# 192 tokens gather their experts and 320 are dense, in a layer whose PEER experts were split 128 to 384; gathered v rows come a token at a time and are summed by TensorE

## The chip, the cores and the metric

The kernel runs on one core of a Trainium2 chip. The metric is the device time of one execution in microseconds, given as the median of several runs; the profile is of one more execution of the same program. Engines are written as in the profile: PE is TensorE (PEld its weight loads), DVE is VectorE, ACT is ScalarE, POOL is GpSimd, SP is SyncE, which issues most DMAs.

## The reference

One decoder layer over 512 tokens of width 2048, in fp32: an adaLN modulation, a combined input projection, 16 RWKV-7 heads beside 16 Mamba-2 heads, an output projection, and then the part that the change is about, a product-key expert network (PEER) with 16384 experts:

```python
q = (xb @ w_query).reshape(PEER_BLOCK, PEER_HEADS, 2, PEER_HALF)
s = jnp.einsum('lhpd,hpnd->lhpn', q, sub_keys)
s_half, i_half = lax.top_k(s, PEER_TOPK)              # 16 of 128 keys, twice per head
cand_s = s_half[:, :, 0, :, None] + s_half[:, :, 1, None, :]
top_s, pos = lax.top_k(cand_s, PEER_TOPK)             # 16 experts per head, 8 heads: 128 per token
gates = jax.nn.softmax(top_s, axis=-1)
act = gelu(jnp.einsum('ld,lhkd->lhk', xb, u_emb[eidx]))
out = jnp.einsum('lhk,lhkd->ld', gates * act, v_emb[eidx])
```

Each token thus uses 128 of 16384 rows of u and of v, each row 2048 fp32 (8 KB). The layer's output is the residual plus the gated result, under a last RMSNorm.

## The kernel before

Tokens lie along the free dimension (`[128, 512]` tiles, 16 of them for the width) up to the experts. Each fp32 product is done as three fp32r matmuls on a high and a low half (`split`, lines 192 and 193: ScalarE casts the high half, GpSimd or VectorE subtracts it for the low one; `mm3`, lines 196 to 198).

The expert part begins near 1340 us. The normalised input `nhi`, `nlo` is made, sixteen query projections run on TensorE, and VectorE finds the top 16 keys and candidates of each head (to about 1640 us). The 512 tokens then go two ways.

The first 384 tokens (`TD`) are dense: all 16384 experts are computed for them and a gate table zeroes the rest. `gate_block` (line 1070) builds the table, 32 tokens at a time: for a token, `J` is a one-hot matrix over 128 experts' second keys, `I2` one over their first keys scaled by the gates, and the matmul of both is the token's 128x128 gate matrix. `J` and `I2` are fp16, with the gate (times 32768) in a high and a low part (`cH`, `cL`), so a matmul has 256 columns; ScalarE copies the high part out of PSUM and VectorE adds the low one. The table goes to HBM (`glD`). `expert_u(i)` (line 1093) computes 128 experts' u products: four loads of 256 KB, each split, 16 times three matmuls of 384 columns, then GELU. The first 38 (`NSP`) are computed ahead and spilled to HBM; they run beside the gate blocks. `expert_v(grp)` (line 1136) multiplies four blocks of experts by their v rows in four quarters `q`: two loads of 512 KB, four splits, 48 matmuls of 384 columns into four of six PSUM accumulators (`po`), which VectorE adds to the residual `hT`. `expert_g` (line 1108) brings the four activations and gate tables together just before. In the value stage one `expert_u` runs after each quarter until all 128 are done, so from the eighth group on the two alternate.

The other 128 tokens are gathered, one per partition. `gather(s)` (line 1173) issues on GpSimd an indirect DMA that fetches for slot `s` one row of u or v for each of the 128 tokens (1 MB). For u, VectorE multiplies the rows by the tokens' inputs and sums along the row (`accum_out`); after 128 slots the weights go through GELU and gates. For v, VectorE adds weight times row to a running sum. There are two buffers `g`. `pace(ins)` (line 1126) is called after every quarter and every `expert_u` and starts as many slots as are due; the 256 slots are spread over 210 such steps (`NGU`). `gathered()` (line 1190) then transposes the sum, adds the residual and writes the normalised output of these tokens.

The order on each engine's queue is written by the framework's planner from a simulated timeline (`schedule_with_timeline_sim=True`); `tc.issue_after(ins)` adds an edge, so that what a block issues on the engine of `ins` comes behind it. Queues run in order. `rms_all` (line 913) is the RMSNorm's sum and root in 128-token pieces.

Of the kernel before, what the change touches and what calls it, by code (L numbers as in the profile page):

```python
# [10 lines left out]
F32 = mybir.dt.float32  # L11
# [8 lines left out]
P = 128  # L20
# [6 lines left out]
TD = 384  # L27
NGU = 210
TB = 32
NACT = 9  # L30
NSP = 38
GSC = 32768.0
# [96 lines left out]
def _hybrid(st, tc, nc, I, out):  # L129
# [100 lines left out]
    sc = st.enter_context(ExitStack())  # L230
    with ExitStack() as sb:
# [599 lines left out]
        def out_open():  # L831
            nonlocal hT, sacc, mq, mods
            hp = st.enter_context(tc.tile_pool(name="hp", bufs=1, side="right", reuse_waits="tile"))
            hT = [hp.tile([P, T], F32, name=f"hT{k}") for k in range(KT)]
            sacc = hp.tile([P, T], F32, name="sacc")
            mq = sb.enter_context(tc.tile_pool(name="mq", bufs=1, side="right", reuse_waits="tile"))
            for d in range(KT):
                nc.sync.dma_start(hT[d], I["xT"][:, d, :])
# [3 lines left out]
        def out_part(q):  # L842
# [20 lines left out]
            for d in range(KT):  # L863
                ps = mm.tile([P, T], F32, name="mm", tag="mm")
                project_to([ps], I["wout"][d:d + 1, :, k0:k1, :], mhi, mlo)
                V.scalar_tensor_tensor(hT[d], ps, mod2[:, d:d + 1], hT[d], OP.mult, OP.add)
                if q == 3:
                    t = mq.tile([P, T], F32, name="a3w", bufs=3) if d else sacc
                    S.activation(t, hT[d], AF.Square)
                    if d:  # L870
                        (V if d % 2 or d > 12 else G).tensor_tensor(sacc, sacc, t, OP.add)
# [3 lines left out]
        hT = sacc = mq = mods = None  # L875
# [37 lines left out]
    def rms_all(psum, tag, pool, acc):  # L913

        n = acc.shape[1] // P
        ps = psum.tile([P, T], F32, name=tag, tag=tag)
        for tt in range(n):
            TE.matmul(ps[:, tt:tt + 1], lhsT=acc[:, P * tt:P * tt + P], rhs=ones[:, 0:1], start=True, stop=True)
# [4 lines left out]
        for tt in range(n):  # L923
            TE.transpose(r[:, P * tt:P * tt + P], rn[:, tt:tt + 1].to_broadcast([P, P]), ident)
        return r[:, 0:acc.shape[1]]


    pu = st.enter_context(tc.tile_pool(name="pu", bufs=2, space=PSUM, reuse_waits="tile"))
    npl = st.enter_context(tc.tile_pool(name="n2", bufs=1, reuse_waits="tile"))
    nhi = [npl.tile([P, T], F32R, name=f"n2hi{k}") for k in range(KT)]  # L930
    nlo = [npl.tile([P, T], F32R, name=f"n2lo{k}") for k in range(KT)]
    glD = dp.tile([TD // TB, P, P, TB], F32, name="glD")
    gt_st = ExitStack()
    gp = gt_st.enter_context(tc.tile_pool(name="gp", bufs=1, reuse_waits="tile"))
    iT = gp.tile([P, T], F32, name="iT")
    jT = gp.tile([P, T], F32, name="jT")
    cH = gp.tile([P, T], F32, name="cH")
    cL = gp.tile([P, T], F32, name="cL")
    va = st.enter_context(tc.tile_pool(name="va", bufs=NACT, side="right", reuse_waits="tile"))

    gq = st.enter_context(tc.tile_pool(name="gq", bufs=1, side="right", reuse_waits="tile"))
    n2t = gq.tile([P, D], F32, name="row")
    ggt = gq.tile([P, P], F32, name="ggt")
    eix = gq.tile([P, P], U32, name="eix")
    with ExitStack() as s3:
        qp = s3.enter_context(tc.tile_pool(name="qp", bufs=2, side="right", reuse_waits="tile"))
        pq = s3.enter_context(tc.tile_pool(name="pq", bufs=2, space=PSUM, reuse_waits="tile"))
        rr = rms_all(pq, "rr", qp, sacc)
        w2 = qp.tile([P, KT], F32, name="w2")
        V.scalar_tensor_tensor(w2, mod2[:, 32:48], 1.0, col("n2w", 0, KT), OP.add, OP.mult)  # L950
        for k in range(KT):
            t = qp.tile([P, T], F32, name="t")
            V.scalar_tensor_tensor(t, hT[k], w2[:, k:k + 1], rr, OP.mult, OP.mult)
# [5 lines left out]
            split(nhi[k], nlo[k], nf, V if k % 4 == 0 else G)  # L959
            if k % 4 == 0:  # L960
                pt = pq.tile([P, 4, P], F32, name="sc")
            TE.transpose(pt[:, k % 4, :], nf[:, TD:T], ident)
            if k % 4 == 3:
                S.copy(n2t[:, P * (k - 3):P * (k + 1)], pt.rearrange("p a b -> p (a b)"))
# [11 lines left out]
        project_to(pss, I["wq"][0:2], nhi, nlo)  # L976
        for h in range(8):
            sv = qp.tile([P, 2, 4, 16], F32, name="sv")
            si = qp.tile([P, 2, 4, 16], F32, name="si")
            for hf in range(2):  # L980
                if h:
                    ps = pu.tile([P, T], F32, name="mm", tag="mm")
                    project_to([ps], I["wq"][2 * h + hf:2 * h + hf + 1], nhi, nlo)
# [60 lines left out]
        V.tensor_copy(ggt, gall[:, 3, :])  # L1044
        ef = qp.tile([P, P], F32, name="ef", bufs=1)
# [211 lines left out]
```

## Time and profile before

| | us |
|---|---|
| median of 3 runs (4144.02 to 4148.79) | 4147.96 |
| profiled execution | 4155.64 |
| its span, first to last instruction | 4153.9 |

| engine | busy us | share of the span |
|---|---|---|
| PE | 3762.3 | 91% |
| PEld | 3248.5 | 78% |
| DVE | 2801.9 | 67% |
| POOL | 2476.5 | 60% |
| ACT | 1346.2 | 32% |
| DMA queue of SP (q1), share of 16 engines | 554.72 MB | 39.8% |
| DMA queue of GpSimd (q0, the gathers) | 268.45 MB | 18.0% |

A busy PE is not PE at its peak: matmuls overlap, and the time from one start to the next is shorter than a matmul's own duration. So the spacing of starts in a timeline is what to read for its speed. The shares are means over stages with different limits; the busy time by stage tells them apart. The mean granted TensorE clock of the execution is 0.942 of 2.4 GHz.

### The profile page before, as it was taken

Reading aid. Unit: us, or ns where it says so; the run is one execution under the profiler, and the core shown is the slowest. Engines: PE = TensorE matmul, PEld = TensorE weight load, DVE = VectorE, ACT = ScalarE, POOL = GpSimd, SP = SyncE. Lnnn points to the kernel's source line nnn. Section 1 sums busy time; section 2 is a strip of 40 time slices with the busy share of each in tenths; the row PEclk is TensorE's granted clock in tenths of the full one; section 3 lists DMA queues with packets and bytes.
Section 4 is the critical chain, followed back from the end, with each engine's and each line's share of the span. In section 5 each row is a group of like instructions: output and inputs, shape, how many; then the busy total and the mean of one; then the engine's idle time right before and its main releaser. Section 6 shows DMA issues by size and latency. Waiting matters only on the chain. (4 is left out here: it accounts for less than half of the span.)

```text
span 4153.9 us, 58305 instructions
## 1 busy us (share of the span) xinstructions
PE 3762.3 (91%) x21094; PEld 3248.5 (78%) x21094; DVE 2801.9 (67%) x5046; ACT 1346.2 (32%) x2566; POOL 2476.5 (60%) x1779
## 2 busy tenths in 40 slices
PE   5899989999999988888898989999999999999998
PEld 3667656766657767677787888999998989989997
DVE  8442245566614899999876678666676766767666
ACT  3443324433323313333322322332323323233323
POOL 5445433433315534334475777878878787878885
PEclk8999999988869998999998999999999999999998
DMA  8455652232342223444586777777777777777773
GB/s 341 166 204 193 203 142 73 77 125 83 107 147 92 81 67 102 154 162 158 198 280 232 248 261 276 266 258 261 268 261 250 271 260 260 264 260 260 269 251 132
DMA packets 358001, 826.89 MB, mean 199 GB/s; under 512 B 54096, under 2 KB 123600, under 8 KB 318672
## 3 DMA queue, kind: packets, MB, share of 16 engines
q1 hardware_dynamic: 320848, 554.72, 39.8%
q0 software_dynamic: 36864, 268.45, 18.0%
q8 instruction: 165, 2.70, 0.3%
q14 instruction: 124, 1.02, 0.1%
HBM read 776.26 MB, written 46.79 MB: 198 GB/s over the span
## 5 line engine op out<-in xcount | busy, mean ns | idle before, releaser
L193 POOL TENSOR_TENSOR wlo<-wr,whi 128x512 fp32r<-128x512 f32 (+2 forms) x832 | 1128.4, 1367 | 1041.5 <-ACT whi L192 920.8
L192 ACT CAST whi<-wr 128x512 fp32r<-128x512 f32 (+2 forms) x832 | 510.7, 617 | 1446.1 <-PE mm L197 829.9
L196 PE MATMUL mm<-n2hi,whi 128*128 128x384 f32 (+1 forms) x2304 | 815.9, 355 | 44.5 <-ACT whi L192 43.1
L198 PE MATMUL mm<-n2hi,wlo 128*128 128x384 f32 (+1 forms) x2304 | 814.7, 354 | 24.0 <-POOL wlo L193 23.8
L197 PE MATMUL mm<-n2lo,whi 128*128 128x384 f32 (+1 forms) x2304 | 810.0, 352 | 3.3 <-POOL n2lo L193 1.7
L193 POOL TENSOR_TENSOR vlo<-vr,vhi 128x512 fp32r<-128x512 f32 x512 | 736.1, 1460 | 120.6 <-ACT vhi L192 113.0
L196 PE MATMUL po<-ghi,vhi 128*128 128x384 f32 x2048 | 700.2, 343 | 68.1 <-DVE hT L1156 43.1
L197 PE MATMUL po<-glo,vhi 128*128 128x384 f32 x2048 | 696.6, 340 | 2.6 <-DVE glo L193 2.6
L198 PE MATMUL po<-ghi,vlo 128*128 128x384 f32 x2048 | 626.6, 347 | 66.2 <-POOL vlo L193 65.8
L1188 DVE SCALAR_TENSOR_TENSOR row<-g,wts,row 128x2048 f32<-128x2048 f32 x127 | 416.0, 3276 | 276.1 <-DMA g<-in_v,eix 275.2
L1180 DVE SCALAR_TENSOR_TENSOR g<-g,row 128x2048 f32<-128x2048 f32 x128 | 409.0, 3200 | 203.9 <-DMA g<-in_u,eix 203.8
L192 ACT CAST vhi<-vr 128x512 fp32r<-128x512 f32 x512 | 310.1, 620 | 624.9 <-PE po L197 492.3
L196 PEld LDWEIGHTS mm<-n2hi,whi 128*128 128x128 f32 x2304 | 448.9, 195 | 65.1 <-ACT whi L192 48.4
L198 PEld LDWEIGHTS mm<-n2hi,wlo 128*128 128x128 f32 x2304 | 447.2, 194 | 56.6 <-POOL wlo L193 39.8
L197 PEld LDWEIGHTS mm<-n2lo,whi 128*128 128x128 f32 x2304 | 448.5, 195 | 20.9 <-issue 5.1
L196 PEld LDWEIGHTS po<-ghi,vhi 128*128 128x128 f32 x2048 | 391.7, 191 | 83.7 <-DVE hT L1156 52.2
L198 PEld LDWEIGHTS po<-ghi,vlo 128*128 128x128 f32 x2048 | 385.0, 194 | 87.2 <-POOL vlo L193 86.9
L197 PEld LDWEIGHTS po<-glo,vhi 128*128 128x128 f32 x2048 | 393.6, 192 | 3.3 <-DVE glo L193 3.3
L1156 DVE SCALAR_TENSOR_TENSOR hT<-po,mod,hT 128x384 f32<-128x384 f32 x512 | 280.0, 605 | 85.0 <-PE po L198 84.7
L1177 POOL DMA_INDIRECT g<-in_v,eix x128 | 202.0, 1578 | 130.7 <-DVE row L1188 80.0
L196 PE MATMUL mm<-nhi,whi 128*128 128x512 f32 x640 | 262.1, 410 | 4.5 <-ACT whi L192 4.5
L198 PE MATMUL mm<-nhi,wlo 128*128 128x512 f32 x640 | 262.5, 410 | 0.0
(414 smaller groups left out, 5318.8 us busy)
## 6 DMA issues: line engine op xcount, KB each, us to landing
wr<-in_uT SPq DMA_DIRECT2D x512, 256.0 KB, 3.6
vr<-in_v SPq DMA_DIRECT2D x256, 512.0 KB, 5.1
wr<-in_wrest SPq DMA_DIRECT2D x160, 256.0 KB, 3.3
aw<-in_ada SPq DMA_DIRECT2D x32, 1024.0 KB, 7.8
a2w<-in_adar SPq DMA_DIRECT2D x64, 512.0 KB, 4.6
glD<-gb SPq DMA_DIRECT2D x12, 2048.0 KB, 7.3
gd<-glD SPq DMA_DIRECT2D x32, 768.0 KB, 8.1
a3w<-in_adar SPq DMA_DIRECT2D x32, 512.0 KB, 3.6
```

The costliest lines, as they stand in the source:

```text
L192: copied.append(S.copy(hi, src))
L193: return (eng or V).tensor_tensor(lo, src, hi.bitcast(F32), OP.subtract)
L196: TE.matmul(ps, lhsT=whi, rhs=xhi, start=first, stop=False)
L197: TE.matmul(ps, lhsT=whi, rhs=xlo, start=False, stop=False)
L198: done_mm[0] = TE.matmul(ps, lhsT=wlo, rhs=xhi, start=False, stop=last)
L1156: V.scalar_tensor_tensor(h, po[d], mod2[:, 48 + k:49 + k], h, OP.mult, OP.add)
L1177: G.indirect_dma_start(out=g, out_offset=None, in_=I["u" if s < P else "v"], in_offset=bass.IndirectOffsetOnAxis(ap=eix[:, n:n + 1], axis=0))
L1180: V.scalar_tensor_tensor(g, g, 1.0, n2t, OP.mult, OP.mult, accum_out=wts[:, n:n + 1])
L1188: V.scalar_tensor_tensor(rows_["o"], g, wts[:, n:n + 1], rows_["o"], OP.mult, OP.add)
```

## The change

`TD` becomes 320, so that 192 tokens (`TG`) are gathered; `NSP` becomes 30, `NGU` 236.

- The residual is held as two sets of tiles, `hT` (320 columns) and `hG` (192 columns, sent to HBM as `hGD` until the end), the normalised input likewise; residual and norm operations are made twice, and a query matmul becomes one of 320 and one of 192 columns.
- u rows are gathered in two sets: 128 slots for the last 128 tokens as before, and 64 slots that serve the other 64 tokens on 128 partitions (two slots' halves at once).
- v rows come a token at a time: one gather of a token's 128 rows, one per partition. After four tokens four `part`s are queued; each is run in `expert_v` after one of the four `i` steps and is four fp32 matmuls of 512 columns in the four column groups of the array (weights broadcast to 32 columns), a copy by ScalarE, and four stores of one row each to HBM (`yG`).
- There are six gather buffers (`NGB`), at most two gathers start in a step, and what was begun in a step is used in the next one. `pace` is also called in the `expert_u` calls ahead of the value stage.
- The gate tables' `J` and `I2` are fp32 with one matmul of 128 columns, and ScalarE's copy alone takes the result out of PSUM.
- PSUM: one bank `pw2` for the parts, five accumulators instead of six; five gate banks instead of three double ones.

```diff
-TD = 384
-NGU = 210
+TD = 320
+NGU = 236
+TG = T - TD
+NGB = 6
-NSP = 38
-GSC = 32768.0
+NSP = 30
...
-                V.scalar_tensor_tensor(hT[d], ps, mod2[:, d:d + 1], hT[d], OP.mult, OP.add)
+                for h, c in ((hT[d], slice(0, TD)), (hG[d], slice(TD, T))):
+                    V.scalar_tensor_tensor(h, ps[:, c], mod2[:, d:d + 1], h, OP.mult, OP.add)
...
+                        mm3(ps[:, 0:TD], whi[:, i, :], wlo[:, i, :], nhi[k], nlo[k], k == 0, False)
+                        mm3(ps[:, TD:T], whi[:, i, :], wlo[:, i, :], ngh[k], ngl[k], False, k == KT - 1)
...
-                J = gx.tile([P, P], F16, name="J", bufs=12)
-                I2 = gx.tile([P, 2, P], F16, name="I2", bufs=12)
+                J = gx.tile([P, P], F32, name="J", bufs=12)
+                I2 = gx.tile([P, P], F32, name="I2", bufs=12)
                 V.tensor_scalar(J, iota, jT[:, t:t + 1], None, OP.is_equal)
-                V.tensor_scalar(I2[:, 0], iota, iT[:, t:t + 1], cH[:, t:t + 1], OP.is_equal, OP.mult)
-                V.tensor_scalar(I2[:, 1], iota, iT[:, t:t + 1], cL[:, t:t + 1], OP.is_equal, OP.mult)
+                V.tensor_scalar(I2, iota, iT[:, t:t + 1], gT[:, t:t + 1], OP.is_equal, OP.mult)
                 TE.matmul(ps[:, i], lhsT=J, rhs=I2, start=True, stop=True)
-            g4 = gb[:, :, 4 * q:4 * q + 4]
-            S.copy(g4, ps[:, :, 0].rearrange("p t i -> p i t"))
-            V.tensor_tensor(g4, g4, ps[:, :, 1].rearrange("p t i -> p i t"), OP.add)
+            S.copy(gb[:, :, 4 * q:4 * q + 4], ps.rearrange("p t i -> p i t"))
...
-    slots = list(range(2 * P))
+    slots = [("u", 0, n) for n in range(P)]
+    for n in range(P):
+        slots += [("u", 1, n // 2)] * (n % 2 == 0) + [("v", 64 + n)]
+    slots += [("v", n) for n in range(64)]
+    nslots = len(slots)
...
         with tc.issue_after(ins.ins):
-            while slots and slots[0] * NGU < units * 2 * P:
-                gather(slots.pop(0))
+            ready, begun[:] = begun[:], []
+            for s in ready:
+                use(*s)
+            while slots and (nslots - len(slots)) * NGU < units * nslots and len(begun) < 2 and held[0] < NGB:
+                begun.append(gather(slots.pop(0)))
...
                     mm3(po[d], vhi[:, cs], vlo[:, cs], *gh[i], i == 0, i == 3)
+                if parts:
+                    parts.pop(0)()
...
+        def part(q):
+            cq = slice(T * q, T * q + T)
+            ps = pw2.tile([P, T], F32, name="pw")
+            for j in range(4):
+                TE.matmul(ps[32 * j:32 * j + 32, :], lhsT=wT[:, t0 + j:t0 + j + 1].to_broadcast([P, 32]), rhs=gs[j][:, cq],
+                          start=True, stop=True, tile_position=(0, 32 * j))
+            ys = vp.tile([P, T], F32, name="ys", bufs=2)
+            S.copy(ys, ps)
+            for j in range(4):
+                nc.sync.dma_start(yG[t0 + j:t0 + j + 1, cq], ys[32 * j:32 * j + 1, :])
+            held[0] -= 4 * (q == 3)
...
     while nu < NSP:
-        expert_u(nu)
+        pace(expert_u(nu))
         nu += 1
     gt_st.close()
-    pv = st.enter_context(tc.tile_pool(name="pv", bufs=6, space=PSUM, reuse_waits="tile"))
+    pv = st.enter_context(tc.tile_pool(name="pv", bufs=5, space=PSUM, reuse_waits="tile"))
```

## Rows read from the trace of the kernel before

**Rows 1.** Busy time by stage: stretch, then each engine's busy us, clock, DMA share, GB/s.
```profile
1400.00:1600.00 200.00, 174.50 (x793) 144.99 (x792) 199.90 (x837) 45.19 (x81) 78.92 (x58) 0.92 0.23 77
1640.00:2064.00 424.00, 355.63 (x2000) 308.76 (x1998) 413.60 (x1245) 144.70 (x261) 170.93 (x133) 0.94 0.46 160
2064.00:4132.00 2068.00, 1902.09 (x10414) 1853.19 (x10415) 1447.35 (x1208) 624.71 (x1117) 1613.32 (x1124) 0.97 0.74 256
```

**Rows 2.** Timeline of TensorE in the value stage: start us, length us, operation.
```profile
2999.72 0.33 PE L196 MATMUL po<-ghi,vhi 128*128 128x384 f32 x1
...
3000.76 0.33 PE L196 MATMUL po<-ghi,vhi 128*128 128x384 f32 x1
```

**Rows 3.** What TensorE waits for, 2800 to 3900 us: total us, times, longest.
```profile
PE po L198 <- POOL vlo L193: 33.9, 26, 5.2
PE mm L198 <- POOL wlo L193: 16.9, 20, 2.1
```

**Rows 4.** GpSimd's costliest groups, 2800 to 3900 us: busy, mean ns; idle before, releasers.
```profile
L193 POOL TENSOR_TENSOR vlo<-vr,vhi 128x512 fp32r<-128x512 f32 x237 | 340.2, 1459 | 5.0 <-ACT vhi L192 3.9
...
L1177 POOL DMA_INDIRECT g<-in_v,eix x107 | 167.6, 1567 | 112.3 <-DVE row L1188 69.8 <-PE po L198 18.6 <-issue 9.0
```

**Rows 5.** The chain that ended last, near its end: start us, us, what.
```profile
4133.31 0.63 DVE hT L1156
```

**Rows 6.** Timeline of TensorE in the query stage, columns as in rows 2.
```profile
1408.18 1.06 PE L990 MATMUL sc<-skT,qT 128*128 128x128 f32 x8
...
1409.31 0.39 PE L197 MATMUL mm<-n2lo,whi 128*128 128x512 f32 x1
...
1410.22 0.39 PE L198 MATMUL mm<-n2hi,wlo 128*128 128x512 f32 x1
```

**Rows 7.** Timeline around one adaLN product in four column groups.
```profile
216.29 0.40 PE L198 MATMUL mm<-nhi,wlo 128*128 128x512 f32 x1
...
216.62 0.64 PE L204 MATMUL a2ps<-a2w,cond 128*32 128x256 f32 x8
...
217.19 0.50 PE L196 MATMUL mm<-nhi,whi 128*128 128x512 f32 x1
```

**Rows 8.** Instructions on the gather buffers `g`: ns min/median/max, first and last start.
```profile
L1180 DVE SCALAR_TENSOR_TENSOR g<-g,row x128: 2274/2522/7655, 2090.8 to 3092.0; 128x2048 f32<-128x2048 f32 x128
...
L1177 POOL DMA_INDIRECT g<-in_v,eix x128: 935/1030/3036, 3087.9 to 4057.5; - x128
L1188 DVE SCALAR_TENSOR_TENSOR row<-g,wts,row x127: 2337/2353/7867, 3102.0 to 4063.6; 128x2048 f32<-128x2048 f32 x127
```

**Rows 9.** Instructions on the tile `iT`, columns as in rows 8.
```profile
L1080 DVE TENSOR_SCALAR I<-iota,iT,cH x384: 296/302/1443, 1639.5 to 2051.9; 128x128 f16<-128x128 f16 x192
...
L1055 ACT COPY iT<-sc x1: 590/590/590, 1631.8 to 1631.8; 128x512 f32<-128x512 f32 x1
```

**Rows 10.** Groups of instructions, 1640 to 2064 us, columns as in rows 4.
```profile
L1080 DVE TENSOR_SCALAR I<-iota,iT,cH 128x128 f16<-128x128 f16 x383 | 154.9, 404 | 0.0
```

**Rows 11.** Instructions of lines 956 and 478, columns as in rows 8.
```profile
L956 DVE TENSOR_SCALAR nf<-t,mod x8: 473/488/1506, 1344.2 to 1372.3; 128x512 f32<-128x512 f32 x8
...
L478 DVE TENSOR_SCALAR M<-d,acs x64: 393/402/410, 226.0 to 371.1; 128x128 f32<-128x128 f32 x64
```

**Rows 12.** Instructions of line 953, columns as in rows 8.
```profile
L953 DVE SCALAR_TENSOR_TENSOR t<-hT,w,rr x16: 739/744/750, 1342.8 to 1369.4; 128x512 f32<-128x512 f32 x16
```

**Rows 13.** DMA, 2800 to 3900 us: queue's packets, MB, share; issues, us to landing.
```profile
q0 software_dynamic: 20827, 151.62, 38.7%
q1 hardware_dynamic: 89641, 136.07, 36.7%
...
g<-in_v,eix POOLq DMA_INDIRECT x107, 7.6
```

**Rows 14.** Transfers of the tiles `act` on SP's queue: issue ns, then landing us.
```profile
L1099 SPq DMA_DIRECT2D actD<-act x38: 319/327/914, 1584.8 to 2054.2; - x38
...
DMA to landing us min/median/max: 1.8/3.5/7.6
```

More of the change, by code (lines that the diff above doesn't have):

```diff
@@ L913, in rms_all @@
     def rms_all(psum, tag, pool, acc):
-        n = acc.shape[1] // P
+        w = acc.shape[1]
+        c0 = [P * i for i in range(w // P)] + [w - P] * (w % P > 0)
+        n = len(c0)
         ps = psum.tile([P, T], F32, name=tag, tag=tag)
-        for tt in range(n):
-            TE.matmul(ps[:, tt:tt + 1], lhsT=acc[:, P * tt:P * tt + P], rhs=ones[:, 0:1], start=True, stop=True)
+        for i, c in enumerate(c0):
+            TE.matmul(ps[:, i:i + 1], lhsT=acc[:, c:c + P], rhs=ones[:, 0:1], start=True, stop=True)
         rn = pool.tile([P, 4], F32, name="rn", bufs=1)
@@ L975, in _hybrid @@
         pss = [pu.tile([P, T], F32, name="mm", tag="mm") for _ in range(2)]
-        project_to(pss, I["wq"][0:2], nhi, nlo)
+        query(pss, 0)
         for h in range(8):
@@ L1162, in expert_v @@
             pace(last)
-            if not slots and not done:
+            if not (slots or begun or parts or done):
                 done.append(True)
@@ new lines, in use @@
+    def use(g, kind, i, n=None):
+        if kind == "u":
+            V.scalar_tensor_tensor(g, g, 1.0, n2s[i], OP.mult, OP.mult, accum_out=wts[i][:, n:n + 1])
+            held[0] -= 1
+            if n == wts[i].shape[1] - 1:
+                weights(i)
+            return
+        four.append((g, i))
+        if len(four) < 4:
+            return
+        gs, t0 = [x[0] for x in four], four[0][1]
+        four.clear()
+        def part(q):
[9 more added lines that the diff above has]
+            held[0] -= 4 * (q == 3)
+        parts.extend(lambda q=q: part(q) for q in range(4))
@@ new lines, in weights @@
+    def weights(i):
+        w = wts[i]
+        S.activation(w, w, AF.Gelu)
+        V.tensor_tensor(w, w, ggt[i], OP.mult)
+        ps = pw2.tile([P, T], F32, name="pw")
+        if i == 0:
+            TE.transpose(ps[:, 0:P], w, ident)
+            S.copy(wT[:, 64:TG], ps[:, 0:P])
+        else:
+            for hs in (slice(0, 64), slice(64, 128)):
+                TE.matmul(ps[hs, 0:64], lhsT=w[hs, :], rhs=ident[hs, hs], start=True, stop=True)
+            S.copy(wT[:, 0:64], ps[:, 0:64])
@@ L1190, in gathered @@
     def gathered():
         acc = sacc[:, TD:T]
[L1193 to L1204 removed]
+        sq = gr.tile([P, D], F32, name="g")
@@ L1213, in _hybrid @@
+            nc.sync.dma_start(out[k][:, TD:T], h)
     NTB = TD // TB
@@ L1230, in _hybrid @@
     for k in range(KT):
[L1231 removed]
+        h = hT[k]
         if k % 4 == 3:
```

182 lines of the change are left out of this document (107 added, 75 removed).

## The prediction

> **What bounds the kernel now.** I read the busy time by stage first [rows 1]. Up to 1640 us the change touches little; VectorE is full there from 1400 on (199.90 of 200 us, the top-16 searches). From 1640 to 2064 us VectorE is full too (413.60 of 424): it builds the gate tables, and TensorE runs the first 38 expert projections beside it. From 2064 to 4132 us TensorE is busy 1902 of 2068 us, GpSimd 1613, VectorE 1447, the DMA engines 0.74 of the time. I call 48 expert matmuls (one `expert_u`, or one quarter of `expert_v`) a unit: 128 + 128 in all, 38 of them ahead of 2064, so 218 after it.
>
> In the timeline six matmuls of 384 columns start from 2999.72 to 3000.76, 0.173 us apart [rows 2]. A unit is 48 x 0.173 = 8.30 us, 218 are 1810 us; the stage takes 2068, a factor of 1.14. The waits show a part of the difference [rows 3]: from 2800 to 3900 us TensorE waits 33.9 + 16.9 us for GpSimd's low halves. GpSimd is late because its gathers stand in line with the splits: a split takes 1.46 us, the issue of a gather 1.57 [rows 4]. So TensorE sets the pace, and GpSimd and the DMA follow closely. The last residual add starts at 4133.31 us [rows 5]; from 4132 to the span's end 22 us of norm and output follow.
>
> **The change, part by part.**
>
> *Columns.* Matmuls of 512 columns start 0.227 us apart (1409.31 to 1410.22, four steps [rows 6]), of 384 columns 0.173: 0.42 ns a column over 13 ns. 320 columns should be 0.147, if nothing else holds a matmul. The weight load does not: fp32 matmuls of 128 columns, each with its own load of 128x128, go 8 in 1.06 us [rows 6], some 0.11 us each when the length of the last is taken off. A unit becomes 7.06 us. 30 units go ahead of the value stage instead of 38, 226 remain: 1596 us.
>
> *Sums on TensorE.* 192 tokens over four stretches of 512 columns, four tokens at a time in column groups: 48 x 4 = 192 sets of four fp32 matmuls. The same form with 256 columns is in the adaLN stage: eight records together from 216.62, the next matmul at 217.19; the 512-column matmul before it, started at 216.29, frees the array at 216.52 by the spacing above [rows 7]. A set of 256 thus costs 0.67 us, entry and exit counted. It is two waves; 256 more columns at 0.42 ns add 0.21 us to each: 1.09 us a set, 209 us in all. Bounds: 0.86 (four passes of columns alone) and 3.5, should the four groups run one after another; the row shows them together, so I take 1.09.
>
> *VectorE.* It loses the 127 weighted sums of 2.35 us at the median and 7.87 at worst, while the u rows grow from 128 to 192 of 2.5 us [rows 8]. The buffers of v are now freed by TensorE. A row is used one pace after its gather began, so VectorE should wait less for landings.
>
> *GpSimd and DMA.* Gathers grow from 256 to 384 of 1.05 MB. Their issue takes 1.03 us at the median, up to 3.04 [rows 8]; 128 more at 1.03 to 1.57 are 132 to 201 us of GpSimd. A unit has 4 x 1.4 + 1.6 x 1.3 = 7.7 us of GpSimd work and 7.06 + 0.9 = 8.0 us of TensorE's: TensorE still leads, by less.
> The Trainium skill (SBUF — State Buffer, section "SBUF: two separate sides") says that GpSimd and a VectorE operation with two SBUF inputs lock each other out of a shared port pair for a whole instruction. The two prices of a gather, three times apart, agree with that, and the sums that go are such operations; by that rule the 192 gathers of v would cost 1.03 instead of 1.57 us, about 100 us less of GpSimd. This is a rival below.
>
> *Gate tables, 1640 us to the value stage.* 384 tokens cost VectorE 414 us now, 1.08 each. After, a token has two fp32 operations of 128 columns and no add. Nearest rows: fp32, 512 columns, one scalar, 0.488 us; fp32, 128 columns out of PSUM, two scalars, 0.402 [rows 11]. I take 0.24 + 0.36, times 1.34 for the stretch that today's operation shows in this stage (0.404 on average [rows 10], 0.302 at the median [rows 9]): 0.80 us, so 192 to 257 us for 320 tokens. TensorE: 25 of the 30 units lie after 1640 (34 of 38 do now), 180 us, and 320 fp32 matmuls of two records, 0.22 us each [rows 6], 72 us: 252. 49 gathers begin in this stage too, with 49 x 2.5 us on VectorE, not all of it ahead of the first value group. I take 320 us, bounds 255 and 400.
>
> *Before 1640 us.* Each query matmul becomes one of 320 and one of 192 columns: 0.147 + 0.11 instead of 0.227, 768 times 0.03 = 23 us, all but the first two projections (3 us) beside the full VectorE of 1400 to 1600 [rows 1]. Residual and norm operations come in two pieces: 0.744 us for 512 columns [rows 12] and 2.353 for 2048 [rows 8] leave 0.21 us that an operation costs beside its columns. Some 32 lie on the path (last output part and norm): 7 us, and 2 more for squares and splits. I take 12 us, bounds 3 and 25.
>
> *Waits added.* A part on TensorE waits for its four gathers (landing 7.6 us at the median [rows 13]), begun one to two units earlier; if one is late, all of TensorE's queue stands. The next part waits for the one bank, thus for ScalarE's copy (0.59 us [rows 9]), that for one of two `ys` tiles, thus for four stores of 2 KB on SP's queue, which stand behind loads that wait for buffers. There are five accumulator banks for six: 0 to 30 us in groups without u units; I count nothing beside the factor.
>
> *Sum.* 1640 + 12, + 320, + (1596 + 209) x 1.14 = 2058, + 22 = 4052 us of span. The profiled execution lies 1.7 us over its span and 7.7 us over the median of the runs: 4052 + 2 - 8 = 4046, and I say **4045**.
>
> **Rivals.**
> *GpSimd is relieved* (VectorE's long sums gone, six gather buffers for two): its gathers wait 69.8 us for those sums in 1100 us now [rows 4]. With a factor of 1.08 and 300 us of gate stage: 1652 + 300 + 1949 + 22 - 6 = 3917. Against: the gathers still stand in line with the splits.
> *The DMA engines bound it.* From 2800 to 3900 us gathers take 38.7% of the time for 151.6 MB, 2.81 us a MB, the rest 36.7% for 136.1 MB, 2.97 [rows 13]. In the 210 units up to the last gather there would be 335 gathers, 351 MB, and 240 MB of loads: 986 + 713 = 1699 us, 8.1 a unit. If no more than 0.85 of the engines can be had that is 1999, and 16 units at 8 follow: 1652 + 320 + 2127 + 22 - 6 = 4115. Against: nothing shows such a ceiling at today's 0.74.
> *Slower: the way of a part's sum out of PSUM.* Place: the third and fourth part of each four tokens. Two `ys` tiles cover two parts, 2 x (12 x 0.147 + 1.09) = 5.7 us. Copy 0.59, four issues of 0.33 on SP, and a landing of 1.8 to 7.6, 3.5 at the median [rows 14]: 5.4 us at the median, just inside; it decides from a landing of 3.8 us on. At 7.6 the pair waits 4 us: 48 x 4 = 192 us with TensorE standing, 4045 + 192 = 4237.
> The Trainium skill (DMA: Bandwidth & Descriptors, "Rules for kernel authors") says that transfers under 64 KB pay mostly overhead; no row has one as small as these, but transfers of 192 KB never land before 1.8 us.
> *The columns are not saved.* A matmul stays at 0.173: (1876 + 209) x 1.14 = 2377, 4365 in all. That needs a floor between 0.11 and 0.17 us; the one slope through two widths speaks against it.
>
> **Chances.** Forecast 0.48 (its own range 3980 to 4110), relief 0.20, DMA 0.17, way out of PSUM 0.12, no saving 0.03. About 0.2% (8 us) is what a measurement of this kernel can tell from no change. Slower: the last two and 0.03 of the DMA's, 0.18; within 0.2%: 0.05; faster: 0.77. Range 3900 to 4190: relief and the DMA case lie in it, of the two slower ones only the milder half of the first.
>
> **What the profile after would show.** Expert matmuls of 320 columns 0.147 us apart; sets of eight records, 1.0 to 1.1 us from entry to the next matmul; the value stage starting near 1970 us, 90 sooner; a DMA share of 0.8 to 0.9; gathers of v nearer 1.03 than 1.57 us. The forecast is wrong if the spacing is above 0.16, if TensorE waits more than 100 us in all at the parts, for gathers or for the `ys` copies, or if the value stage is over 2130 us long.

## The result, and the profile after

The kernel after takes 4295.84 us (median of 4 runs, 4291.74 to 4301.42), the kernel before 4145.99 in the same comparison: a ratio of 1.037 (1.034 to 1.039). It is 3.7% slower; 4045 was predicted. The profiled execution took 4301.42 us, its span is 4299.7.

Busy time by stage (columns as in [rows 1]); the third line is the same stretch as the third there:

```profile
1640.00:2064.00 424.00, 327.40 (x1877) 302.62 (x1876) 329.53 (x724) 115.44 (x211) 216.71 (x154) 0.86 0.71 253
2064.00:4132.00 2068.00, 1927.24 (x11877) 1615.20 (x11877) 1102.47 (x1034) 696.65 (x1274) 1563.06 (x1200) 0.97 0.81 290
4132.00:4299.00 167.00, 106.80 (x523) 69.59 (x523) 47.91 (x100) 41.08 (x83) 45.19 (x40) 0.69 0.38 136
```

The first stage is no shorter though VectorE has 84 us less to do in it. In the second TensorE is as busy as before and the DMA engines are at 0.81 for 0.74. The third stretch has no counterpart: before, the span ended 20 us after 4134.

TensorE's timeline (start, length, in us), which answers to [rows 2] and [rows 7]:

```profile
3004.56 0.31 PE L197 MATMUL po<-ghi,vhi 128*128 128x320 f32 x1
3004.71 0.30 PE L198 MATMUL po<-glo,vhi 128*128 128x320 f32 x1
3004.94 1.06 PE L1245 MATMUL pw<-g,wT 128*32 128x512 f32 x8
3005.94 0.41 PE L199 MATMUL po<-ghi,vlo 128*128 128x320 f32 x1
```

Matmuls of 320 columns start 0.147 us apart, and from the matmul ahead of a set to the one behind it are 1.23 us, 1.08 more: both terms of the forecast are there to 0.01 us. So TensorE's work for a unit did fall, from 8.30 us to 7.06 and, where sets lie, 1.08 for each. The time of a unit did not. I read it from VectorE's last residual add of group 12 to that of group 28, 128 units with u and v in turn: 2791 to 3977 us before, **9.27 us a unit**; 2849 to 4042 after, **9.32**. The stretch ahead of it, from the value stage's start, and this stretch itself (columns as in [rows 1]):

```profile
2066.00:2849.00 783.00, 669.85 (x4022) 605.21 (x4021) 545.05 (x504) 231.61 (x427) 623.18 (x440) 0.93 0.81 290
2849.00:4042.00 1193.00, 1170.34 (x7329) 946.51 (x7326) 534.75 (x487) 433.23 (x791) 880.97 (x710) 1.00 0.81 291
```

In the second of them TensorE is busy for 98% of the time at the full clock. Its 139 sets stand there in 214 pieces (a piece is what lies between two matmuls of the experts), and a piece of one matmul costs as much as a set of four. The first set of all starts at 2602 us, so most of the first stretch has none.

VectorE's groups from 1640 to 2064 us (busy, mean ns; idle before, and what ended it), where [rows 10] has tables alone:

```profile
L1116 DVE TENSOR_SCALAR I<-iota,iT,gT 128x128 f32<-128x128 f32 x314 | 145.0, 462 | 0.0
L1115 DVE TENSOR_SCALAR J<-iota,jT 128x128 f32<-128x128 f32 x313 | 118.6, 379 | 0.0
L1230 DVE SCALAR_TENSOR_TENSOR g<-g,row 128x2048 f32<-128x2048 f32 x49 | 117.4, 2415 | 94.5 <-DMA g<-in_u,eix 94.5
```

The tables' operations cost 0.84 us a token (0.80 forecast). These durations overlap: VectorE's busy time without the products is 329.53 - 117.4 = 212 us for 314 tokens, 0.68 each, to be held against the 1.08 before. But 49 products of u rows stand among them, and VectorE, in order, idles another 94.5 us for rows that have not landed: another 212 us in all.

The DMA of 2800 to 3900 us, for [rows 13]:

```profile
q0 software_dynamic: 25589, 186.34, 44.8%
q1 hardware_dynamic: 87899, 137.15, 37.3%
```

The longest waits of the same stretch (total us, times, longest):

```profile
ACT vhi L193 <- PE po L198: 264.3, 139, 8.6
DVE act L1155 <- ACT act L1128: 258.5, 43, 14.2
DVE hT L1197 <- PE po L199: 187.4, 59, 12.9
...
ACT whi L193 <- DMA wr<-in_uT: 70.0, 24, 8.0
POOL g L1225 <- DVE g L1230: 67.4, 23, 4.7
...
DVE g L1230 <- DMA g<-in_u,eix: 48.3, 16, 10.5
```

No line of PE itself is among them down to 10 us; TensorE's waits for GpSimd's low halves [rows 3] are gone in this stretch. Earlier they are not: from 2064 to 2700 us they are 70 us,

```profile
PE po L199 <- POOL vlo L194: 51.0, 31, 4.3
...
PE mm L199 <- POOL wlo L194: 18.6, 10, 4.2
```

where the kernel before has 26:

```profile
PE po L198 <- POOL vlo L193: 23.9, 17, 4.2
...
PE mm L198 <- POOL wlo L193: 1.9, 3, 1.1
```

The chain that ended last, in order of time (start, us, what), for [rows 5]:

```profile
4150.84 7.66 DMA g<-in_v,eT
...
4169.98 10.33 DMA g<-in_v,eT
...
4191.92 3.85 DMA yG<-ys
4196.09 4.74 DMA g<-yG
...
4229.04 3.49 DMA wr<-in_uT
4232.60 0.67 issue
4233.31 1.27 POOL wlo L194
...
4280.45 1.85 ACT gd L1200 x4
```

The last gathers, one after another, the store and reload of the sums and the gathered tokens' end come first, and only then the last four `expert_u` and group 31, alone.

### The profile page after: what moved, and what is told of

It reads as the page before. It is cut to its first block, busy times and chain, and to the rows that moved or that the text cites. A ratio compares the mean times of both kernels' runs of the same rounds, so it can differ in the third digit from the quotient of the medians.

```text
span 4299.7 us, 64989 instructions
## 1 busy us (share of the span) xinstructions
PE 3870.1 (90%) x23694; PEld 3119.5 (73%) x23694; DVE 2414.9 (56%) x4523; ACT 1427.3 (33%) x2780; POOL 2507.4 (58%) x1919
## 4 chain that ended last, share of the span: by engine, by line
PE 63%; DVE 17%; DMA 8%; POOL 5%; issue 3%; ACT 1%; SPq 0%; POOLq 0%; DVEq 0%; ACTq 0%
PE mm L199 9%; PE mm L197 9%; PE mm L198 9%; PE pw L1245 7%; PE po L197 6%; PE po L199 6%; PE po L198 6%; DVE I L1116 3%; DVE g L1230 2%; DMA wr<-in_uT 2%; DVE J L1115 2%; POOL vlo L194 2%; POOL wlo L194 1%; DMA AI<-abD 1%; POOL g L1225 1%
## 5 line engine op out<-in xcount | busy, mean ns | idle before, releaser
L197 PE MATMUL mm<-n2hi,whi 128*128 128x320 f32 x2304 | 756.8, 329 | 53.7 <-ACT whi L193 52.9
L199 PE MATMUL mm<-n2hi,wlo 128*128 128x320 f32 x2304 | 751.9, 328 | 52.8 <-POOL wlo L194 52.6
L198 PE MATMUL mm<-n2lo,whi 128*128 128x320 f32 x2304 | 741.6, 322 | 0.0
L197 PE MATMUL po<-ghi,vhi 128*128 128x320 f32 x2048 | 646.5, 322 | 50.6 <-DVE hT L1197 43.5
L198 PE MATMUL po<-glo,vhi 128*128 128x320 f32 x2048 | 640.4, 316 | 0.5 <-DVE glo L194 0.5
L199 PE MATMUL po<-ghi,vlo 128*128 128x320 f32 x2048 | 565.5, 320 | 51.2 <-POOL vlo L194 51.0
L1197 DVE SCALAR_TENSOR_TENSOR hT<-po,mod,hT 128x320 f32<-128x320 f32 x512 | 250.8, 542 | 389.4 <-PE po L199 389.4
L1155 DVE TENSOR_TENSOR act<-gd,act 128x320 f32<-128x320 f32 x128 | 214.1, 1687 | 422.4 <-ACT act L1128 392.2
L1245 PE MATMUL pw<-g,wT 128*32 128x512 f32 x1536 | 327.2, 631 | 31.2 <-DMA g<-in_v,eT 21.3
L1225 POOL DMA_INDIRECT g<-in_u,eix x192 | 247.8, 1291 | 93.7 <-PE pw L1245 23.8
```

The source lines that it names most:

```text
L197: TE.matmul(ps, lhsT=whi, rhs=xhi, start=first, stop=False)
L198: TE.matmul(ps, lhsT=whi, rhs=xlo, start=False, stop=False)
L199: done_mm[0] = TE.matmul(ps, lhsT=wlo, rhs=xhi, start=False, stop=last)
L1155: V.tensor_tensor(a.rearrange("p (b t) -> p b t", t=TB), gd[:, :, i, :], a.rearrange("p (b t) -> p b t", t=TB), OP.mult)
L1197: V.scalar_tensor_tensor(h, po[d], mod2[:, 48 + k:49 + k], h, OP.mult, OP.add)
L1225: G.indirect_dma_start(out=g, out_offset=None, in_=I[s[0]], in_offset=bass.IndirectOffsetOnAxis(ap=ix, axis=0))
```

## The experiments

Each ratio is to runs of the kernel before on the same chip (their medians there 4135 to 4140 us); no_early_gathers is a single run. "Unit" is the time of a unit between the ends of groups 12 and 28, "start" the last residual add of group 0 (before: 2117 and 9.27; after: 2115 and 9.32). In the first four runs theory A is that the order of TensorE's queue, the place of `gathered()` and the gathers put ahead cost the time, and not columns or sets.

**1. Order.** The 192 sets stand in TensorE's queue in some 290 pieces, of which a single costs as much as a set of four. whole_sets ties the four matmuls of a part together:

```diff
+            def one(j):
+                return TE.matmul(ps[32 * j:32 * j + 32, :], lhsT=wT[:, t0 + j:t0 + j + 1].to_broadcast([P, 32]),
...
+            with tc.issue_after(one(3).ins):
+                for j in range(3):
+                    one(j)
```

> Only the order of one part's four matmuls is tied: the one on the newest token's rows goes first, the other three stand right behind it in TensorE's queue. In the changed kernel 192 sets stand in TensorE's queue in some 290 pieces (131 fours, 39 pairs, 104 singles), and each piece costs 1.08 us, a single as much as a four. Theory A (the order of the queue costs the time): about 100 pieces fewer, 100 us less, near 4195 us. Theory B (the DMA and the gathers bound the value stage, TensorE only fills its time with pieces): TensorE waits for gathers instead, 4270 to 4310 us.

4289.32 us, 1.038 (1.033 to 1.042), no gain in sum. Between the ends of groups 12 and 28 the pieces fell from 214 to 144:

```profile
2852.00:4013.00 1161.00, 1104.82 (x7287) 948.42 (x7286) 552.42 (x488) 427.75 (x783) 859.90 (x702) 0.98 0.82 295
```

TensorE's busy time there fell by 66 us, the stretch by 32 (1193 to 1161): idle gaps grew from 23 to 56 us and the clock fell from 1.00 to 0.98. Group 28 ends 29 us sooner, but the last residual add only 10 (4272 for 4282), since the end of the gathered tokens comes first there too, and its last gather begins only 10 us sooner (4160 for 4170). So the pieces are worth some 30 us of the stage, not the 100 of theory A, and nearly nothing in sum. gathered_last calls `gathered()` behind the last group and no longer from within group 29, ahead of the last four projections:

```diff
-            if not (slots or begun or parts or done):
-                done.append(True)
-                gathered()
...
+    assert not (slots or begun or parts)
+    gathered()
```

> Only the place of gathered() changes: after the last group instead of ahead of the last expert_u calls. Theory A: in the changed kernel its ten PSUM tiles come ahead of those of the last four expert_u calls, which with group 31 run alone at the end (4127 to 4281 us for 8 units that are worth some 60); now they run beside the last gathers, and gathered() (some 30 us) follows: 50 to 80 us less, near 4230 us. Theory B (the gathers' arrival ends the kernel anyway, at 4180 us, and the rest only follows): 4270 to 4300 us.

4261.97 us, 1.032 (1.028 to 1.037): group 31 ends at 4200 for 4281, but the gathers then end the kernel, and 34 us are left of 81 (20 by the ratios). whole_last is both edits, the base for what follows:

> Both the tied sets and gathered() last. Theory A: the gains add up, some 160 us, near 4130 us, a little under the kernel before (4146). Theory B: 4250 to 4300 us.

4243.36 us, 1.027 (1.022 to 1.031); unit 9.06. The last residual add comes at 4168 us, and the gathers still end the kernel, 73 us later.

**2. No gathers beside the tables.** no_early_gathers takes the pace from the projections ahead (and NGU to 206); the gathered tokens' end is left out of it.

```diff
-        pace(expert_u(nu))
+        expert_u(nu)
```

> No gathers ahead of the value stage (expert_u is not followed by pace there, NGU 206 for 236); the end of the kernel will be worse, as more gathers are left for it. Read is the stage from 1640 us to the first value group. Theory A (gathers hold it: 66 us of VectorE between the gate operations, and landings of the u loads stretched by their traffic): the first quarter of the value stage is done near 2000 us instead of 2082. Theory B (30 expert_u calls and their loads set the stage, whose ring of three buffers turns no faster): 2060 to 2085 us again. The whole: 4300 to 4400 us by either.

4267.45 us. The first quarter is done at 1955 us for 2082, the 30th gelu at 1939 for 2057: the gathers held the stage of the tables by some 120 us. But a unit takes 9.33 us as before, and the gathers now end the kernel at 4254. tables_first adds whole sets, a part after each load of a projection, and the gathered tokens last (NGU 200):

```diff
+                if pop is not None and pop:
+                    pop.pop(0)()
```

> Whole sets, gathered tokens last, no gathers ahead of the first value group (200 for the pace, so up to two a unit), and a part also after each of the four loads of a projection, so that the buffers of v come free in every unit and not in every second; what gathers remain are done behind the last group. By the run without gathers ahead the value stage starts 120 us sooner (first quarter at 1955 us). If the gathers keep to the units then (384 in 226 units, 1.7 a unit, 8.7 to 9.1 us landing, six buffers) and the pace is 9.3 to 9.5 a unit: 4110 to 4150. Theory D: the same bytes in 120 us less want 0.87 of the DMA engines; at 0.82 and 296 GB/s 640 MB take 2160 us from 1950, and the time is 4140 to 4190. Theory P: more parts at once, no gain from their place: as D or worse, 4200 and over.

4305.51 us, 1.042 (1.038 to 1.045); unit 9.68, with the DMA engines at 0.84 and 301 GB/s from 2700 to 4000 us. Here what leaves the tables' stage comes back in the value stage and at the end, which is 132 us behind the last residual add.

**3. Rows or parts.** quarter_rows fetches a quarter of each v row, quarter_parts sums one of four stretches, quarter_both does both.

```diff
+        vq = I["v"].rearrange("e (a c) -> (e a) c", c=T)
+        G.indirect_dma_start(out=g[:, 0:T] if s[0] == "v" else g, out_offset=None, in_=vq if s[0] == "v" else I["u"], ...
...
+            if q:
+                held[0] -= 4 * (q == 3)
+                return
```

> Base: the version with whole sets and the gathered tokens finished last, 4243 us, 9.3 us a unit from 2700 to 4010 us. Here a gather of v fetches a quarter of each row (2 KB instead of 8 KB, 0.26 MB instead of 1.05 MB a gather), as many descriptors, issues, sets, copies and stores as there; the sums of the gathered tokens are thus made from the wrong columns. Theory D (the transfers set the pace: 0.82 of the DMA engines at 296 GB/s in that stretch): 192 x 0.79 = 151 MB less, which is 510 us at 296 GB/s; not all of it is on the path, and TensorE's columns are next at about 8.2 us a unit, so the stretches with v gathers fall to 8.0 to 8.7 us a unit and the time to 4030 to 4150. Theory P (the way of a part over TensorE, ScalarE and the stores sets the pace): 4225 to 4245, the pace stays above 9.1.

> Same base, 4243 us. Here only the first of the four stretches of columns of each four tokens is summed: 48 sets, copies to ys and 192 stores instead of 192, 192 and 768; the gathers are all there, and the gathered tokens' sums repeat the first stretch. Theory P: TensorE loses 144 x 1.08 = 156 us, ScalarE and the stores three quarters of theirs, and the buffers of v come free three parts earlier: 4050 to 4110, 8.4 to 8.7 us a unit between 2700 and 4010. Theory D: the transfers are the same 640 MB, so the pace stays at 9.0 to 9.3 and the time at 4190 to 4240 (the end of the chain of gathers alone gets 10 to 40 us shorter).

> Base: whole sets and gathered tokens last, 4243 us; here a quarter of each v row is fetched (2 KB) and one of the four stretches of columns is summed, as in the two runs that did one of both and moved nothing (4246 each). Two limits side by side (transfers with late landings, TensorE's own work with the sets; each holds when the other is gone): with both gone a unit falls to 8.0 to 8.6 us between 2700 and 4010 us, time 4020 to 4120. A third limit that neither touches (VectorE, which stands in line for rows of u and for the gelu while residual adds wait; GpSimd's line of splits and gathers): 9.0 to 9.4 us a unit, 4190 to 4250.

4245.89 us (unit 9.39) and 4245.80 (9.43): either alone gains nothing in sum against 4243, so both theories as I had put them fell. By stage both do something: the span ends 17 us behind the last residual add for 73, and a unit is 0.33 and 0.37 us longer than the 9.06 of whole_last (which the expectation had at 9.3). Why a unit grew no run shows. Both together: 4061.59 us, 0.982 (0.977 to 0.986), unit 8.38. TensorE's longest waits from 2700 to 4000 us, of quarter_rows:

```profile
PE po L197 <- DVE hT L1198: 97.7, 26, 5.1
```

and of quarter_parts:

```profile
PE pw L1245 <- DMA g<-in_v,eT: 54.3, 27, 5.5
PE po L197 <- DVE hT L1197: 51.2, 14, 5.4
PE mm L197 <- ACT whi L193: 32.9, 15, 3.7
```

With the parts cut, TensorE waits for landings (0.81 of the DMA engines, 293 GB/s, in that run); with the bytes cut, it does its own work (7.06 + 1.08 a unit) and waits for VectorE's adds. Cuts that give 0, 0 and together 182 us speak for two limits side by side; which two they are is read from the waits and not tested further.

**4. One part of the change alone, in the kernel before.** gates_alone has fp32 tables; narrow_alone computes only 320 of the 384 dense columns.

```diff
+                I2 = gx.tile([P, P], F32, name="I2", bufs=12)
...
-            V.tensor_tensor(g4, g4, ps[:, :, 1].rearrange("p t i -> p i t"), OP.add)
```

```diff
+TN = 320
...
-        last = project_to([ps[:, 0:TD]], I["uT"][i:i + 1], ndhi, ndlo)
+        last = project_to([ps[:, 0:TN]], I["uT"][i:i + 1], ndhi, ndlo)
```

> The kernel before with one part of the change alone: the gate tables in fp32 (no halves, no add, copy on ScalarE); 384 dense tokens, 38 projections beside the tables, no gathers there. The step of the prediction for this part: VectorE 384 x 0.80 = 307 us instead of 414; TensorE 34 x 8.3 = 282 + 384 x 0.22 = 84, 366 us; so the stretch from 1640 to 2064 us gets 45 to 60 us shorter and the time is 4075 to 4105. The rival (the table stage was held by something other than VectorE's table operations): 4130 to 4150.

> The kernel before with the columns of the change alone: the expert products, the gelu, the factors and the residual adds work on 320 of the 384 dense columns (64 tokens get no experts); tables, 38 projections ahead, 256 gathers and the weighted sums on VectorE as before. The prediction's step (TensorE's columns set the pace, factor 1.14): 218 units x (8.30 - 7.06) x 1.14 = 308 us less, about 3830. Theory S (a supply of 9.2 to 9.4 us a unit sets the pace, at 384 columns and at 320: 9.27 in the kernel before from 2791 to 3977 us, 9.25 to 9.41 in the runs with a quarter of the parts or of the rows): 4040 to 4130, and a unit still takes 8.9 to 9.3 us in that stretch.

gates_alone: 4131.78 us, 1.000 (0.998 to 1.002). The busy time of 1640 to 2064 us in it:

```profile
1640.00:2064.00 424.00, 398.06 (x2405) 379.41 (x2404) 227.69 (x733) 150.56 (x270) 195.09 (x147) 0.99 0.54 187
```

VectorE falls from 413.60 to 227.69 us, more than forecast, but TensorE has 398 us there: it was next, close behind. The start moved from 2117 to 2086, and the median shows nothing of it; the profiled execution of the kernel before was 8 to 20 us over its medians, so the 31 may be too many.

narrow_alone: 4079.58 us, 0.985 (0.981 to 0.988); unit 8.86 (the profiled run). **The columns by themselves are worth 60 us, not 308**: theory S held, with a unit just under its 8.9. From the end of group 0 to that of group 31 it is 96 us (1922 for 2018), but two gathers then begin behind the last residual add, and the span ends 47 us after it for 18. TensorE's waits from 2700 to 4000 us:

```profile
PE po L199 <- POOL vlo L194: 120.1, 51, 5.7
PE mm L199 <- POOL wlo L194: 41.8, 36, 3.8
PE po L197 <- DVE hT L1157: 27.7, 15, 3.5
```

The two waits of [rows 3], 59 us in this stretch before, grow to 162, and the mean clock is 0.94 for 0.98. GpSimd stands 191 us in that stretch with a gather, splits behind it in its line, for one of the two buffers that VectorE still reads.

**5. What the gathers cost.** dense_only leaves them all out; fewer_gathers keeps 256 of 384; short_products multiplies 64 of 2048 columns of u; issues_only fetches quarter rows of both kinds.

```diff
+    slots.clear()
```

```diff
-        slots += [("u", 1, n // 2)] * (n % 2 == 0) + [("v", 64 + n)]
-    slots += [("v", n) for n in range(64)]
+        slots += [("v", 64 + n)]
```

```diff
+            V.scalar_tensor_tensor(g[:, 0:64], g[:, 0:64], 1.0, n2s[i][:, 0:64], OP.mult, OP.mult, accum_out=...)
```

> Same base, without the 384 gathers and all that is done with them (no rows of u on VectorE, no parts; the end of the gathered tokens takes other rows). What is left is the dense stage of 320 columns, at 148 GB/s if a unit took 7.06 us. If the gathers' presence (their line on GpSimd, VectorE's waits and products, their transfers) is what holds the stage: first quarter at 1950 to 1970 us, then 7.4 to 8.2 us a unit, time 3700 to 3850. If the dense chain itself (load, ScalarE's copy, GpSimd's low half, TensorE, with two or three buffers each) is the supply: 8.8 to 9.3 us a unit and 3990 to 4100.

> Base: whole sets and gathered tokens last, 4243 us. Here only 128 of the 192 tokens gather their experts (256 gathers for 384, 128 sets for 192; the other 64 get wrong rows at the end), spread over the same 236 units. If each gather costs its share of the 657 us between this base and the run without gathers (1.71 us each): 128 x 1.71 = 219 us less, 4000 to 4050. If a limit is passed (fewer than some 1.1 gathers a unit leave TensorE alone with 7.06 + 0.6 x 1.08 us): more than that, 3880 to 3970. If only the 64 sets that go count, 69 us: 4160 to 4190.

> Same base, all gathers, sets and waits as there, but VectorE's product of a gathered row of u takes 64 of the 2048 columns (about 0.15 us for 2.29; the weights are thus wrong), 411 us of VectorE less. Theory V (VectorE's line holds the table stage and the residual adds): the first quarter 40 to 90 us sooner, VectorE's wait for the gelu with the adds behind it no longer, time 4060 to 4150. Theory T (transfers and their landings; VectorE would only wait longer in the same places): first quarter 0 to 40 us sooner, time 4190 to 4245.

> Same base, with 384 gathers of quarter rows of u and of v (0.26 MB each), products of u on 512 columns and 48 sets: what stays in full are GpSimd's 384 issues, 0.95 us each and 0.3 before the next one. If bytes, landings and products are the cost: no gather is then late, a unit takes 7.2 to 7.8 us, first quarter at 1960 to 2010, time 3640 to 3760 (3586 without any gather, 48 sets x 1.08 = 52). If GpSimd's line is the cost (4 x 1.28 + 1.63 x 1.25 = 7.2 us a unit beside TensorE's 7.06 + 0.3): 8.2 to 8.8 us a unit, 3850 to 3980.

| kernel | us | ratio to before | start | groups 1 to 12 | unit | end |
|---|---|---|---|---|---|---|
| whole_last | 4243.36 | 1.027 (1.022 to 1.031) | 2113 | 736 | 9.06 | 73 |
| short_products | 4090.24 | 0.990 (0.987 to 0.993) | 2076 | 641 | 8.77 | 94 |
| fewer_gathers | 3998.96 | 0.967 (0.964 to 0.970) | 2059 | 702 | 8.44 | 17 |
| issues_only | 3767.02 | 0.911 (0.908 to 0.914) | 2023 | 620 | 7.65 | 17 |
| dense_only | 3586.25 | 0.867 (0.864 to 0.870) | 1983 | 549 | 7.04 | 17 |

"Groups 1 to 12" is the time in us from the last residual add of group 0 to that of group 12, "end" the time from the last residual add of all to the end of the span.

Without gathers a unit takes 7.04 us, TensorE's columns and nothing else, less than the 7.4 to 8.2 expected. The value stage of dense_only (columns as above):

```profile
2064.00:3540.00 1476.00, 1471.12 (x9997) 1466.38 (x9996) 518.69 (x709) 582.57 (x1051) 1099.05 (x829) 1.00 0.52 159
```

So a load, ScalarE's copy, GpSimd's low half and two or three buffers of each keep up with 7.04 us. The 384 gathers with their sums cost 657 us of the kernel, 1.7 each; the 128 that the change adds, with 64 of its sets, cost 244, 1.9 each. Not all of it lies in the value stage: of the 244 (246 in the profiled executions) 55 lie ahead of the end of group 0, 135 from there to the last residual add, and 57 at the end, where the gathers are no longer last. Of the 657 the start has 130 and the end 56. VectorE's time in the products is 153 us of the 657, and more than half of that, 95, lies in groups 1 to 12. With all 384 issues left but a quarter of the bytes, products and parts, 476 of the 657 us are gone. For GpSimd's issues at most the other 181 remain, with 48 sets (52 us) and the rest of the bytes and products among them.

**6. The lag of the projections.** In whole_last VectorE stands 239 us from 2700 to 4000 us at the product of gate and act, with residual adds behind it. more_ahead has 12 tiles for 9 and goes further ahead:

```diff
-NACT = 9
+NACT = 12
...
-            if nu < min(128, 4 * grp + 12):
+            if nu < min(128, 4 * grp + 15):
```

> Same base, with 12 tiles act for 9 and projections up to 15 ahead of the group for 12. In the base VectorE stands 239 us from 2700 to 4000 us at the product of gate and act, each time for a gelu that has just been done, with residual adds behind it in its line; TensorE waits 25.9 us for these adds there, VectorE's waits for rows of u are 86. If this line is what keeps the pace at 9.1: VectorE's wait for the gelu falls under 60 us, a unit to 8.5 to 8.9 and the time to 4150 to 4215. If it only fills time that VectorE has: 4230 to 4255.

4218.62 us, 1.019 (1.016 to 1.022), 25 us less, but VectorE still waits 228.5 us for the gelu and a unit takes 9.23. The last projection ends at 4045 us for 4091; the theory that this line keeps the pace fell.

**7. A kernel that beats both.** four_buffers is gates_alone with four gather buffers, and a row is used one pace after its gather began.

```diff
-    gr = st.enter_context(tc.tile_pool(name="gr", bufs=2, ...
+    gr = st.enter_context(tc.tile_pool(name="gr", bufs=4, ...
...
+            ready, begun[:] = begun[:], []
+            for x in ready:
+                use(*x)
```

> The kernel before with fp32 tables (4132 us), and four gather buffers for two, a row used one pace after its gather began (the room comes from keeping the query's 128 columns apart from the 384); 384 dense tokens and weighted sums on VectorE as before. If GpSimd's waits for the two buffers (98 + 39 us from 2700 to 4000 us) were what kept a unit at 9.3 for 8.30 of columns: TensorE's waits for low halves (62 us there) go, 8.7 to 9.0 us a unit, 4030 to 4095. If transfers kept it: 4110 to 4145.

4098.26 us, 0.992 (0.989 to 0.994), unit 9.07. GpSimd's wait for a buffer, in gates_alone from 2700 to 4000 us:

```profile
POOL g L1170 <- DVE row L1181: 97.7, 38, 6.0
...
POOL g L1170 <- DVE g L1173: 39.2, 14, 4.7
```

is gone; of four_buffers, 2700 to 3850 us, the longest that stands before a gather is

```profile
POOL g L1185 <- issue: 16.8, 91, 0.3
```

That was worth 34 us; a unit still takes 0.77 us more than TensorE's 8.30. early_rows then paces the gathers from the first projection on (NGU 244), early_rows_30 has 30 projections ahead for 38:

```diff
-        expert_u(nu)
+        pace(expert_u(nu))
...
-NSP = 38
+NSP = 30
```

> four_buffers (384 columns, 128 tokens, fp32 tables, 4098 us) with its gathers paced from the first projection on, over 244 units: some 39 gathers of u with 39 x 2.4 = 94 us of VectorE lie in the stage of the tables, where VectorE is busy 207 of 414 us and TensorE 395. If they are hidden there, the value stage starts within 20 us of 2099 and has 39 gathers fewer: at 1.9 us each 74 us less, 4020 to 4060. If they hold the tables as in the change's kernel (120 us for 49): first quarter at 2150 to 2200, time 4095 to 4150.

> The same with 30 projections ahead of the value stage for 38: TensorE then has 30 x 8.3 + 84 = 333 us in the stage of the tables, VectorE 207 + 31 x 2.4 = 281. If TensorE ends that stage: first quarter near 2030, eight more units of 9.1 us behind it, time within 15 us of early_rows. If VectorE ends it: up to 30 us later than early_rows.

4108.90 us, 0.992 (0.990 to 0.995): the start comes 73 us later, at 2172, and a unit falls to 8.69, which is no gain in sum. With 30: 4061.02 us, 0.980 (0.978 to 0.983), start 2086, unit 8.69. It is 2% faster than the kernel before, the fastest of those that do the whole computation, and 48 us under early_rows, where neither theory had it; VectorE's wait for rows in the stage of the tables is 81 us for 133. VectorE in early_rows_30, 1650 to 2100 us:

```profile
L1192 DVE SCALAR_TENSOR_TENSOR g<-g,row 128x2048 f32<-128x2048 f32 x33 | 78.2, 2371 | 80.8 <-DMA g<-in_u,eix 80.8
```

## Why the prediction was wrong

Three terms of its sum (4052 us of span, 4299.7 measured) are off, by 90, 76 and 78 us; with 4 us ahead of 1640 that is the whole difference.

- **The gate stage, 320 us: +90.** The value stage began at 2066 us, not near 1972. The prediction counted 49 x 2.5 us of products and put a part of them elsewhere. It missed that a paced product stands in VectorE's line ahead of tables, and that VectorE waits there for the landing (94.5 us more). no_early_gathers shows it: without these gathers the first quarter came 127 us sooner. The tables themselves were priced too high, by durations that overlap: 0.68 us of VectorE a token for 0.80.
- **The value stage, (1596 + 209) x 1.14: +76** for the 218 units that were done by 4127 us. The prices of a matmul and of a set were right. The step that failed is "So TensorE sets the pace": the factor was taken to scale with TensorE's work, and narrow_alone shows that it is a second limit: 1.24 us less of columns gave 0.41 us a unit and 60 us in all. Six buffers lifted that limit (GpSimd's line) from 2800 us on, as the prediction half expected, and 128 more gathers put others in its place: 135 us of the stage (behind group 0) for what the sum charged as 64 sets, 80 us with the factor. By stretch the excess lies ahead of the sets. Up to the end of group 12 some 79 units and 26 sets are 668 us by the forecast, and they took 783, with TensorE busy 670; short products alone make groups 1 to 12 95 us shorter, so VectorE's products of u rows hold them up by that much, by themselves or by what they delay. In the mixed groups behind them 1.14 even gave the right pace (139 sets in 128 units there: (7.06 + 1.09 x 1.09) x 1.14 = 9.40, measured 9.32), but by accident: TensorE is busy there 98% of the time, as the sum's 139 sets are 214 pieces, some 80 us more than it charged.
- **The end, 22 us after the last unit: +78.** At 4127 us eight units were left, 73 us by the forecast's pace; they took 154 because the gathered tokens' end stood ahead of the last four projections in program order. No step of the prediction asked what stands behind `gathered()`. gathered_last regained 34 us (20 by the ratios).
- **Before 1640 us:** 12 forecast, 16 measured at the first gelu (1584 to 1600): right.

The rivals. *The DMA bound* came nearest in kind: the share is 0.81, inside the 0.8 to 0.9 named, and the gathers' bytes are one of the two things that only cut together gave time back (quarter_both). Its ceiling of 0.85 was mine; short_products ran at 0.90 and 332 GB/s from 2100 to 2700 us. *The way out of PSUM* gave 4237, the nearest number, for the wrong reason: TensorE's waits for `ys` are 9.9 us from 4040 us on, and cutting three quarters of the copies and stores alone gained nothing. *GpSimd is relieved* is true of the waits from 2800 us on, not of those before 2700, and of a gather's issue (0.96 us for v rows on average from 2800 to 3900 us, 1.57 before); more buffers alone were worth 34 us (four_buffers), not 130. *The columns are not saved* was wrong as a mechanism. Of the marks named in advance, the spacing, the sets and the DMA share came out; the start of the value stage did not, and its length, 2066 to 4281, was over the 2130 named.

What stays open: how the 135 us that the added gathers cost in the value stage divide between VectorE's products and the transfers, and why a unit grew when bytes or parts alone were cut. The shares found by cutting one at a time do not add up.

## What to carry to other kernels

A stage that runs 14% over its busiest engine's work may have a second limit that close: here 15% less of that work made a unit 4% shorter. So find and price the second limit before moving work onto it (here a gather: 1.7 to 1.9 us of the kernel). When one cut alone gains nothing, look at each stage, since a gain in one can be lost in another, and cut two at once before dropping either. Work paced into an in-order queue takes its wait along: ask what stands behind it in program order, in the middle and at the end.

## What the runs showed of the hardware

*VectorE held by GpSimd.* The product of gate and act has a median of 494 ns in the kernel after and a longest of 7122 from 2700 to 4000 us. One case, in quarter_parts (start, length), VectorE:

```profile
3312.57 5.58 DVE L1155 TENSOR_TENSOR act<-gd,act 128x320 f32<-128x320 f32 x1 [10.34 <-ACT act L1128]
```

and GpSimd:

```profile
3311.64 1.28 POOL L194 TENSOR_TENSOR wlo<-wr,whi 128x512 fp32r<-128x512 f32 x1
3312.88 1.26 POOL L194 TENSOR_TENSOR vlo<-vr,vhi 128x512 fp32r<-128x512 f32 x1
3314.11 2.48 POOL L194 TENSOR_TENSOR wlo<-wr,whi 128x512 fp32r<-128x512 f32 x2
3316.56 1.25 POOL L194 TENSOR_TENSOR vlo<-vr,vhi 128x512 fp32r<-128x512 f32 x1
```

VectorE's operation begins during GpSimd's first subtraction and ends 0.3 us after the fifth; they follow one another without a gap. The Trainium skill (SBUF — State Buffer, "SBUF: two separate sides") says that a VectorE operation with two SBUF inputs and a GpSimd operation that reads SBUF exclude each other for the whole of an instruction. The row agrees, and shows that the wait can last a row of them.

*A single matmul of a column group* between matmuls of the whole array cost as much as four groups together: from 2700 to 4010 us of the kernel after 87 singles took 1.07 us at the median over the normal spacing, 112 fours 1.09. The Trainium skill (TensorEngine Tiling (Array Packing), "Key Properties") says that changing the tiling mode drains the array; the trace agrees. Still, tying the fours together took 32 us off the stretch of groups 13 to 28 and next to nothing off the whole, since TensorE's time was not the only limit.
